# A gated MLP and a Mamba-2 mixer on one core: the skip weights' load, the order of the last stage, and four small moves

## The chip, the cores and the metric

The kernel runs on one core of one Trainium2 chip. The metric is the device time of one execution in microseconds (us). A core has five engines, each with its own queue of instructions that it works off in order: TensorE (PE; its weight loads are PEld), VectorE (DVE), ScalarE (ACT), GpSimd (POOL) and SyncE (SP). They wait for each other through semaphores. SP, ACT and POOL also issue DMA transfers.

## What is computed

Two layers over h of 1024 tokens by 1024 channels, then a last RMS norm. All is float32. The matmuls are split: each operand is written as a high and a low part, and three products (high times high, high times low, low times high) replace one.

```
h = x
# layer 0: chunked causal spatial gating
z, u, v = split(rmsnorm(h) @ a_w_in)            # 1024 -> 3 x 2048
mixed   = causal(w_s) applied per chunk of 128 to layernorm(v), + b_s
h       = h + (u * mixed * silu(z)) @ a_w_out
# layer 1: Mamba-2
z, xbc, dt = split(rmsnorm(h) @ b_w_in)         # 2048, 4096, 32 columns
x, B, C = split(silu(causal_conv(xbc)))         # 32 heads of 64, 8 groups of 128
dt      = softplus(dt + dt_bias);  dA = cumsum(dt * A) within each chunk
y       = diagonal part + part carried over chunks + x * d_skip   # d_skip: one number per head
h       = h + rmsnorm_per_group(y * silu(z)) @ b_w_out
out     = rmsnorm(h) * final_norm_w             # mean over 1024 channels, per token
```

## The kernel before

The kernel is one long program written out in order for all engines. In each stretch under `manual_schedule` every engine gets its instructions in the order of the code; where one stretch meets the next, instructions of both interleave. TensorE does nearly everything as blocks of 128x512 products.

**Seven products in place of eight.** Every large product is cut in four quarters and done with Strassen's form in Winograd's variant: seven products, numbered 1 to 7, of sums of the quarters. `Block` does this for columns of the two input projections, `Wide` for the columns of v, `Out` for the two output projections. The sums of weight quarters are `t1` and `t2` in `Block`; they are built by DMA transfers that add to their destination (`accum_op`), which POOL issues (`add`). `sums_a` starts `t2`, and `sums_b` goes on with `t1` and `t2`. Product 4 and 6 use `t2`, product 5 uses `t1`. `prep` casts an operand to its high part on ScalarE (`wh`, `xh`, `yh`) and subtracts on VectorE to get the low part (`wl`, `xl`, `yl`); `mm` multiplies; `post` takes the accumulators out of PSUM.

**First layer's start.** `head` normalizes x and does the first half of v's columns, `rest` the second. Between them some small parameters are loaded by SP: `hv` (decay bias and rate) and `dsk`, the skip weights of the 32 heads spread so that partition p holds head 2c + p//64 at column c. In `rest`, `mix_a` loads the mixing weights `ws`; `mix_b` transposes them on TensorE into `wc` (tag k2, four buffers, which the `vt` rows of v use too, until their stores to `v_d` have landed); `mix_c` multiplies ones by `wc` (L877). `mix_b` runs within the sixth product and `mix_c` ahead of the seventh.

**Decays.** `decays` is a generator. `blocks` calls it once in each unit of the second layer's projection, a unit being one of two halves of a product, until it ends. It holds VectorE's steps for softplus and the cumulative sums, ScalarE's exponentials, eight small stores by POOL, and four transposes on TensorE, among them those of `last`. Other work in a unit comes before its step.

**Output projections.** `Out.product` runs one of the products 1, 2, 7, 6, 4, 5 in four steps c of 24 matmuls; a hook adds the loads and sums of each step. `plus` sums on VectorE, `add` by a DMA. Rows are kept in halves of 512 channels, in `u`. `square` lets ScalarE sum the squares of a half row into `stats`. For the left half (nb 0), VectorE then scales that sum and adds the norm's small constant, one 128x1 step per row block (L1253). `rstd_half` and `rstd_a` add the right half's share, and POOL raises to the power -1/2; `rstd_b` refines it on VectorE. `ao` is the first layer's output, `bo` the second's.

**The end.** After product 5, `into_end` does product 3 of `bo` in four blocks of 24 matmuls, `last_mm(0)` to `last_mm(3)`, over operands that `prep_unit` splits. `post(3, tt)` adds the block to the rows (0, tt) and squares them. `finish_b(th, tt, rs)` scales the left half on ScalarE (already weighted, `weigh_left`), the right half on VectorE (with weights in the same step), and SP stores both. Rows (1, tt) were summed in product 5 and need only finishing, with `r1`.

Of the kernel before, what the change touches and what calls it, by code (L numbers as in the profile page):

```python
# [8 lines left out]
F32 = mybir.dt.float32  # L9
# [20 lines left out]
def kernel(  # L30
# [152 lines left out]
    class Block:  # L183
# [33 lines left out]
        def sums_b(self):  # L217
            nc.scalar.mul(self.t1, self.b[0, 0], -1.0)
            self.add(self.t1, 0, 1)
            self.add(self.t2, 1, 1)  # L220

# [606 lines left out]
    with tc.manual_schedule():  # L828
        second = head()
        hv = cst.tile([P, 4], F32, name="hv")  # L830
        nc.sync.dma_start(out=hv[0:32, 0:1], in_=b_dt_bias[0].rearrange("(h o) -> h o", o=1))
        for q in range(4):
            nc.sync.dma_start(out=hv[q * 32:(q + 1) * 32, 1:2], in_=b_a_log[0].rearrange("(h o) -> h o", o=1))
        dsk = cst.tile([P, 16], F32, name="dsk")
        dskv = b_d_skip[0].rearrange("(c f) -> f c", f=2)
        for f in range(2):
            nc.sync.dma_start(out=dsk[f * 64:(f + 1) * 64, :], in_=dskv[f].partition_broadcast(64))
        nA = hv[:, 2:3]
        nc.scalar.activation(nA, hv[:, 1:2], AF.Exp)
        nc.vector.tensor_scalar(nA, nA, -1.0, None, ALU.mult)  # L840
# [148 lines left out]
    class Out:  # L989
# [256 lines left out]
        def square(self, th, tt, nb):  # L1246
# [4 lines left out]
            nc.scalar.activation(junk, self.row(th, tt, nb), AF.Square, accum_out=ss[:, nb:nb + 1])  # L1251
            if nb == 0:
                nc.vector.tensor_scalar(ss[:, 0:1], ss[:, 0:1], 1.0 / D, NORM_EPS, ALU.mult, ALU.add)  # L1253

# [31 lines left out]
    def hook_a(n, c):  # L1286
# [11 lines left out]
        else:  # L1298
            ao.prep_last(c)
            store_h1(1, c, 0)  # L1300

# [280 lines left out]
    def decays():  # L1582
# [5 lines left out]
        yield  # L1588
        yield
        nc.scalar.activation(e_, e_, AF.Exp)  # L1590
        yield
# [31 lines left out]
        for q in range(4):  # L1623
# [4 lines left out]
            if q % 2:  # L1628
                yield
        tk = s8([P, 2048], "tk")  # L1630
        tok = tk[:, 0:768].rearrange("p (v c r) -> p v c r", v=3, c=2)
        decb = tk[:, 768:1024]
        last = k1([P, 256], "last")
        for j in range(2):
            nc.scalar.copy(out=last[:, j * P:(j + 1) * P],
                           in_=ecs[:, j * P + P - 1:j * P + P].broadcast_to([P, P]))
        tps = []
        for two in ((dt, dte), (cs, last)):
# [490 lines left out]
    def hook_b(n, c):  # L2129
# [18 lines left out]
        elif n == 2:  # L2148
# [12 lines left out]
            if c:  # L2161
                (bo.plus if c < 3 else bo.add)(bo.a(0, 0, c - 1), bo.a(1, 0, c - 1))
        elif n == 7:
# [28 lines left out]
        elif n == 5:  # L2192
            bo.prep_last(c)
            if c:
                weigh_left((c - 1) // 2, 2 * ((c - 1) % 2))
            if c == 3:
                bo.prep_unit(0)

    def finish_b(th, tt, rs):
        l, r = bo.row(th, tt, 0), bo.row(th, tt, 1)  # L2200
        nc.scalar.activation(l, l, AF.Identity, scale=rs)
        (nc.scalar if (th, tt) == (0, 3) else nc.sync).dma_start(out=outr[th * 4 + tt][:, 0:512], in_=l)
        nc.vector.scalar_tensor_tensor(r, r, rs, end["fnwb"][:, 512:], ALU.mult, ALU.mult)
        nc.sync.dma_start(out=outr[th * 4 + tt][:, 512:], in_=r)
# [226 lines left out]
    def into_end():  # L2431
# [5 lines left out]
        r1 = bo.rstd_half(1)  # L2437
        for tt in range(4):
            bo.last_mm(tt)
            if 0 < tt < 3:  # L2440
                bo.prep_unit(tt + 1)
            if tt:
                bo.post(3, tt - 1)
                bo.rstd_a(0, tt - 1)
            finish_b(1, tt, r1[:, tt:tt + 1])
            if tt:
                finish_b(0, tt - 1, bo.rstd_b(0, tt - 1))
        bo.post(3, 3)
        bo.rstd_a(0, 3)
        finish_b(0, 3, bo.rstd_b(0, 3))  # L2450

# [31 lines left out]
```

## Time and profile before

| what | value |
|---|---|
| runs | 1481.75, 1481.93, 1485.11 us (median 1481.93) |
| profiled execution | 1481.93 us, span from first to last instruction 1480.2 us |
| TensorE busy | 1452.0 us, 98% of the span, 7202 matmuls |
| VectorE, ScalarE, GpSimd busy | 1041.8 us (70%), 784.1 us (53%), 404.5 us (27%) |
| mean granted TensorE clock | 0.996 of full speed |
| DMA | 257.52 MB, mean 174 GB/s |

The profile is of one execution. Its page gives busy times, the chain of work that ended last, and the costliest groups of instructions. Further views answer questions: waits (who stood idle until whom), a timeline of one engine, windows (busy times in stretches of time), and the DMA issues with their times to landing. In a row, "[6.84 <-ACT wc L871]" means that the engine stood 6.84 us before this instruction and that the last thing it waited for was ScalarE's write of `wc` on line 871. Matmuls are pipelined, so their shown durations (0.39 us) overlap; the next starts after about 0.23 us.

### The profile page before, as it was taken

The page shows a single profiled execution, that of the slowest core. Times are in us where ns is not written, and L with a number is a line of the kernel's source. Part 1 is how long each engine was busy: PE and PEld are TensorE (multiplying, and loading weights), DVE is VectorE, ACT ScalarE, POOL GpSimd, SP SyncE. Part 2 cuts the span into 40 slices and gives each one's busy share as a digit, 9 for nine tenths or more (in the row PEclk, how much of TensorE's full clock was granted, in tenths as well). Part 3 has the DMA queues.
Part 4 walks back from the last instruction along what each step waited for, and adds up shares of the span by engine and source line. Part 5 has one row for each costly group of instructions (what it writes and reads, how often), then busy time and mean ns, then how long its engine had stood idle before and what let it go on. Part 6 is the DMA issues. An engine that isn't in the chain of part 4 may idle for free. (4 is left out here: it accounts for less than half of the span.)

```text
span 1480.2 us, 20005 instructions
## 1 busy us (share of the span) xinstructions
PE 1452.0 (98%) x7202; PEld 1196.5 (81%) x7202; DVE 1041.8 (70%) x1713; ACT 784.1 (53%) x1261; POOL 404.5 (27%) x451
## 2 busy tenths in 40 slices
PE   9998999999999999999999999999999999999997
PEld 7786888888888888887788888888888888787875
DVE  7864666776666655678665558767787777788976
ACT  7632333222323445565665646657677766866463
POOL 2101110000000023202122323205676767742221
PEclk9999999999999999999999999999999999999999
DMA  8653423332322999957467988786777566699963
GB/s 287 128 171 91 165 91 120 105 120 94 116 85 78 341 265 252 258 132 175 120 159 169 197 163 162 156 248 158 203 185 201 176 190 141 192 282 282 271 115 114
DMA packets 174549, 257.52 MB, mean 174 GB/s; under 512 B 16513, under 2 KB 98673, under 8 KB 171250
## 3 DMA queue, kind: packets, MB, share of 16 engines
q1 hardware_dynamic: 124128, 171.55, 37.7%
q0 software_dynamic: 42688, 70.79, 24.2%
q10 hardware_dynamic: 7634, 13.90, 2.6%
q8 instruction: 57, 0.93, 0.3%
q14 instruction: 42, 0.34, 0.1%
HBM read 187.19 MB, written 51.18 MB: 161 GB/s over the span
## 5 line engine op out<-in xcount | busy, mean ns | idle before, releaser
L134 PE MATMUL acc<-hh,wh 128*128 128x512 f32 x868 | 339.7, 391 | 0.7 <-ACT u L297 0.7
L136 PE MATMUL acc<-hh,wl 128*128 128x512 f32 x868 | 338.3, 390 | 0.4 <-DVE wl L112 0.3
L135 PE MATMUL acc<-hl,wh 128*128 128x512 f32 x868 | 337.8, 389 | 0.0
L136 PEld LDWEIGHTS acc<-hh,wl 128*128 128x128 f32 x868 | 162.9, 188 | 35.7 <-DVE wl L112 1.6
L134 PEld LDWEIGHTS acc<-hh,wh 128*128 128x128 f32 x868 | 163.1, 188 | 34.3 <-ACT u L297 1.1
L135 PEld LDWEIGHTS acc<-hl,wh 128*128 128x128 f32 x868 | 163.0, 188 | 33.0
L112 DVE TENSOR_TENSOR wl<-wr,wh 128x1024 fp32r<-128x1024 f32 (+1 forms) x81 | 96.2, 1188 | 105.8 <-ACT wh L111 105.6
L111 ACT CAST wh<-wr 128x1024 fp32r<-128x1024 f32 (+1 forms) x97 | 99.3, 1025 | 78.7 <-PE acc L135 58.7
L297 ACT COPY u<-acc 128x512 f32<-128x512 f32 x93 | 53.9, 582 | 148.0 <-PE acc L136 147.9
L134 PE MATMUL ab<-hh,wh 128*128 128x512 f32 x288 | 122.2, 424 | 0.0
L136 PE MATMUL ab<-hh,wl 128*128 128x512 f32 x288 | 113.2, 393 | 0.0
L135 PE MATMUL ab<-hl,wh 128*128 128x512 f32 x288 | 112.5, 391 | 0.6 <-DVE hl L112 0.6
L134 PE MATMUL acc<-wh,hh 128*128 128x512 f32 x216 | 85.6, 396 | 0.3 <-DVE vt L396 0.3
L135 PE MATMUL acc<-wl,hh 128*128 128x512 f32 x216 | 84.3, 390 | 1.0 <-DVE wl L364 1.0
L136 PE MATMUL acc<-wh,hl 128*128 128x512 f32 x216 | 84.1, 389 | 0.0
L976 POOL DMA_DIRECT2D y_d<-y x8 | 4.4, 550 | 287.2 <-DVE y L973 287.2
L1949 ACT ACTIVATE wl<-wl,tk 128x128 f32<-128x128 f32 x256 | 81.6, 392 | 0.3 <-DMA wl<-cs_d 0.2
L1967 DVE TENSOR_TENSOR wl<-wl,cw 128x512 f32<-128x512 f32 x64 | 61.0, 965 | 16.2 <-ACT wl L1951 15.1
L112 DVE TENSOR_TENSOR xl<-ya,xh 128x1024 fp32r<-128x1024 f32 x36 | 44.8, 1243 | 37.6 <-ACT xh L111 32.4
L1162 PE MATMUL bo<-wl,xh 128*128 128x512 f32 x192 | 64.2, 392 | 1.3 <-DVE stats L1253 0.7
L134 PEld LDWEIGHTS ab<-hh,wh 128*128 128x128 f32 x288 | 54.4, 189 | 13.3 <-issue 5.7
L111 ACT CAST xh<-ya 128x1024 fp32r<-128x1024 f32 x36 | 37.7, 1048 | 49.8 <-PE ao L1162 35.0
(331 smaller groups left out, 3236.4 us busy)
## 6 DMA issues: line engine op xcount, KB each, us to landing
wr<-in_a_w_in_dram SPq DMA_DIRECT2D x32, 512.0 KB, 3.6
wl<-cs_d SPq DMA_DIRECT2D x64, 256.0 KB, 5.4
wr<-in_b_w_in_dram SPq DMA_DIRECT2D x30, 512.0 KB, 4.3
wb<-in_a_w_out_dram SPq DMA_DIRECT2D x10, 1024.0 KB
wb<-in_b_w_out_dram SPq DMA_DIRECT2D x10, 1024.0 KB, 9.4
wr<-in_b_w_in_dram SPq DMA_DIRECT2D x36, 256.0 KB, 5.3
wide<-in_a_w_in_dram SPq DMA_DIRECT2D x16, 512.0 KB, 7.3
v<-v_d SPq DMA_DIRECT2D x8, 1024.0 KB
```

The costliest lines, as they stand in the source:

```text
L111: nc.scalar.copy(out=hi, in_=src)
L112: return (eng or nc.vector).tensor_tensor(out=lo, in0=src, in1=hi.bitcast(F32), op=ALU.subtract)
L134: nc.tensor.matmul(out=o, lhsT=l[0], rhs=r[0], start=start, stop=False, **kw)
L135: nc.tensor.matmul(out=o, lhsT=l[0], rhs=r[1], start=False, stop=False, **kw)
L136: nc.tensor.matmul(out=o, lhsT=l[1], rhs=r[0], start=False, stop=stop, **kw)
L297: nc.scalar.copy(out=self.u[n][:, i], in_=a)
L976: store = lambda: nc.gpsimd.dma_start(out=y_d[-1], in_=y)
L1162: nc.tensor.matmul(out=o[i], lhsT=X[x_][:, k, i * P:(i + 1) * P], rhs=Y[y_][:, k, :], start=not more and c == 0 and k == 0 and x_ == y_, s ...
L1949: nc.scalar.activation(wl[:, j, :], wl[:, j, :], AF.Relu, scale=-1.0, bias=tokc(2, c, self.g)[:, j:j + 1])
L1967: V.tensor_tensor(out=wl, in0=wl, in1=self.cw[c][:, 640:768].unsqueeze(1).broadcast_to([P, 4, P]), op=ALU.mult)
```

## The change

Six places change.

1. `sums_b` issues the second sum into `t2` before the sum into `t1`.
2. The skip weights come as one row of 32 numbers, broadcast to all partitions (`skip`), and two VectorE copies take every second one into `dsk`, instead of two DMA loads.
3. In `Out`, the scaling of the left half's mean is one step for four row blocks (`mean`), called in the second and third step of product 5, instead of one step per row block.
4. `decays` waits one unit more before its first exponential, and copies `last` one unit before the transposes; its two temporary tiles are allocated a unit later.
5. In the second product of `bo`, the sum of the third step goes by DMA (`add`) instead of on VectorE (`plus`), as that of the fourth does.
6. `into_end` is written out without its loop, with another order of the finishing, squaring and splitting, and the last right half is multiplied by the norm's weights before its root is known.

```diff
         def sums_b(self):
             nc.scalar.mul(self.t1, self.b[0, 0], -1.0)
+            self.add(self.t2, 1, 1)
             self.add(self.t1, 0, 1)
-            self.add(self.t2, 1, 1)
...
+        skip = cst.tile([P, 16, 2], F32, name="skip")
+        nc.sync.dma_start(out=skip.rearrange("p c f -> p (c f)"), in_=b_d_skip[0].partition_broadcast(P))
         dsk = cst.tile([P, 16], F32, name="dsk")
-        dskv = b_d_skip[0].rearrange("(c f) -> f c", f=2)
         for f in range(2):
-            nc.sync.dma_start(out=dsk[f * 64:(f + 1) * 64, :], in_=dskv[f].partition_broadcast(64))
+            nc.vector.tensor_copy(out=dsk[f * 64:(f + 1) * 64, :], in_=skip[f * 64:(f + 1) * 64, :, f])
...
             nc.scalar.activation(junk, self.row(th, tt, nb), AF.Square, accum_out=ss[:, nb:nb + 1])
-            if nb == 0:
-                nc.vector.tensor_scalar(ss[:, 0:1], ss[:, 0:1], 1.0 / D, NORM_EPS, ALU.mult, ALU.add)
+
+        def mean(self, th):
+            v = stats[:, th * 4:th * 4 + 4, int(self.keep), 0]
+            nc.vector.tensor_scalar(v, v, 1.0 / D, NORM_EPS, ALU.mult, ALU.add)
...
             ao.prep_last(c)
+            if c in (1, 2):
+                ao.mean(c - 1)
...
         yield
         yield
+        yield
         nc.scalar.activation(e_, e_, AF.Exp)
...
-        tk = s8([P, 2048], "tk")
-        tok = tk[:, 0:768].rearrange("p (v c r) -> p v c r", v=3, c=2)
-        decb = tk[:, 768:1024]
         last = k1([P, 256], "last")
...
+        yield
+        tk = s8([P, 2048], "tk")
+        tok = tk[:, 0:768].rearrange("p (v c r) -> p v c r", v=3, c=2)
+        decb = tk[:, 768:1024]
         tps = []
...
-                (bo.plus if c < 3 else bo.add)(bo.a(0, 0, c - 1), bo.a(1, 0, c - 1))
+                (bo.plus if c < 2 else bo.add)(bo.a(0, 0, c - 1), bo.a(1, 0, c - 1))
...
             bo.prep_last(c)
+            if c in (1, 2):
+                bo.mean(c - 1)
...
-        nc.vector.scalar_tensor_tensor(r, r, rs, end["fnwb"][:, 512:], ALU.mult, ALU.mult)
+        if weighed is None:
+            nc.vector.scalar_tensor_tensor(r, r, rs, end["fnwb"][:, 512:], ALU.mult, ALU.mult)
+        else:
+            nc.vector.tensor_scalar(r, weighed, rs, None, ALU.mult)
...
-        for tt in range(4):
-            bo.last_mm(tt)
-            if 0 < tt < 3:
-                bo.prep_unit(tt + 1)
-            if tt:
-                bo.post(3, tt - 1)
-                bo.rstd_a(0, tt - 1)
-            finish_b(1, tt, r1[:, tt:tt + 1])
-            if tt:
-                finish_b(0, tt - 1, bo.rstd_b(0, tt - 1))
+        bo.last_mm(0)
+        bo.prep_unit(2)
+        bo.last_mm(1)
+        bo.post(3, 0)
+        bo.rstd_a(0, 0)
+        finish_b(1, 0, r1[:, 0:1])
+        bo.prep_unit(3)
+        finish_b(0, 0, bo.rstd_b(0, 0))
+        bo.last_mm(2)
+        bo.post(3, 1)
+        finish_b(1, 1, r1[:, 1:2])
+        bo.rstd_a(0, 1)
+        finish_b(1, 2, r1[:, 2:3])
+        finish_b(0, 1, bo.rstd_b(0, 1))
+        bo.last_mm(3)
+        bo.post(3, 2)
+        bo.rstd_a(0, 2)
+        finish_b(1, 3, r1[:, 3:4])
+        finish_b(0, 2, bo.rstd_b(0, 2))
         bo.post(3, 3)
+        left = k2([P, 512], "left")
+        nc.vector.tensor_tensor(out=left, in0=bo.row(0, 3, 1), in1=end["fnwb"][:, 512:], op=ALU.mult)
         bo.rstd_a(0, 3)
-        finish_b(0, 3, bo.rstd_b(0, 3))
+        finish_b(0, 3, bo.rstd_b(0, 3), left)
```

More of the change, by code (lines that the diff above doesn't have):

```diff
@@ L2197, in hook_b, with finish_b @@
                 bo.prep_unit(0)
-    def finish_b(th, tt, rs):
+    def finish_b(th, tt, rs, weighed=None):
         l, r = bo.row(th, tt, 0), bo.row(th, tt, 1)
```

## The prediction, made before the change was run

> **What bounds the kernel now.** I read the page's busy shares, then the stages, then TensorE's waits, then the queues around the longest of them.
>
> ```profile
> PE 1452.0 (98%) x7202; PEld 1196.5 (81%) x7202; DVE 1041.8 (70%) x1713; ACT 784.1 (53%) x1261; POOL 404.5 (27%) x451
> ```
> ```profile
> 100.00:200.00 100.00, 93.16 (x405) 75.38 (x405) 65.82 (x122) 29.77 (x42) 16.95 (x22) 0.97 0.38 126
> ```
> ```profile
> PE tp L877 <- ACT wc L871: 6.8, 1, 6.8
> ...
> PE bo L1162 <- DVE stats L1253: 0.7, 1, 0.7
> ...
> PE acc L134 <- ACT u L297: 0.7, 1, 0.7
> ...
> PE bo L1162 <- DVE wl L1069: 0.4, 1, 0.4
> PE tp L1643 <- ACT last L1635: 0.4, 1, 0.4
> ...
> PE acc L136 <- DVE wl L112: 0.3, 1, 0.3
> ```
>
> TensorE is busy for 1452.0 of 1480.2 us, so only what it stands idle, what it runs at a lower clock, and what follows its last matmul can be won; an instruction saved elsewhere counts only where TensorE waits for it. One stretch stands out, 100 to 200 us, with 6.84 us idle and a mean clock of 0.97. The waits name 6.8 us at once at the matmuls of `mix_c` (L877); each other wait that the change touches is under 1 us. What follows the last matmul is read below, at the part on the end.
>
> Around L877, in the order of the queues (SP, POOL, ACT, DVE, PE), and the DMA beside it:
>
> ```profile
> 117.40 1.40 SPq L837 DMA_DIRECT2D dsk<-in_b_d_skip_dram  x2
> ```
> ```profile
> 123.78 0.69 POOL L397 DMA_DIRECT2D v_d<-vt  x1 [0.69 <-DVE vt L396]
> ```
> ```profile
> 139.75 1.23 ACT L871 COPY wc<-tp 128x512 f32<-128x512 f32 x2 [20.62 <-DMA v_d<-vt]
> ```
> ```profile
> 141.97 1.22 DVE L364 TENSOR_TENSOR wl<-wide,wh 128x1024 fp32r<-128x1024 f32 x1 [15.43 <-ACT wh L360]
> ```
> ```profile
> 127.06 1.03 PE L869 MATMUL tp<-ident,ws 128*128 128x128 f32 x8
> ...
> 132.94 0.39 PE L135 MATMUL acc<-wl,hh 128*128 128x512 f32 x1
> 133.16 0.39 PE L136 MATMUL acc<-wh,hl 128*128 128x512 f32 x1
> 140.39 3.73 PE L877 MATMUL tp<-wc,ones 128*128 128x512 f32 x4 [6.84 <-ACT wc L871]
> ...
> 144.19 0.40 PE L135 MATMUL acc<-wl,hh 128*128 128x512 f32 x1
> ```
> ```profile
> 137.00:139.00 2.00, 0.00 (x0) 0.00 (x0) 0.00 (x0) 0.00 (x0) 0.00 (x0) 0.53 0.79 301
> ```
> ```profile
> 118.80:137.00 18.20, 14.75 (x70) 11.96 (x68) 7.60 (x15) 0.20 (x1) 2.82 (x4) 1.00 0.05 0
> ```
> ```profile
> v_d<-vt POOLq DMA_DIRECT2D x4, 256.0 KB, 19.1
> ...
> hv<-in_b_a_log_dram SPq DMA_DIRECT2D x4, 0.1 KB, 2.1
> ```
> ```profile
> v_d<-vt POOLq DMA_DIRECT2D x16, 256.0 KB, 3.2
> ```
>
> The windows give the share of the DMA engines and GB/s last, the clock ahead of them. SP issues the skip weights' two loads at 117.4 to 118.8: 4 KB each, but source elements that do not lie side by side, so 2 x 64 x 16 = 2048 pieces of 4 bytes. From 118.8 to 137 the DMA engines are busy for a share of 0.05 and move 0 GB/s to the digit. The four 256 KB stores of `vt` that POOL issues by 124.5 take 19.1 us to land; over the whole run such a store takes 3.2. `wc` is written over the buffers of these `vt` (tag k2), so ScalarE stands 20.62 us, copies at 139.75, and TensorE, out of work at about 133.4, starts L877 at 140.39, at a clock of 0.50 from about 137.
>
> **The change, part by part.**
>
> *The skip row.* Two loads of 4-byte pieces go; one load of 128 rows of 128 bytes (32 heads, side by side) and two VectorE copies of 64x16 come. The nearest row for such pieces is the load of the 32 decay columns at L1365, 1024 pieces of 128 bytes:
>
> ```profile
> DMA packets 1073, 0.16 MB, mean 127 GB/s; under 512 B 1040, under 2 KB 1073, under 8 KB 1073
> ```
>
> 1040 packets under 512 B, those 1024 among them, pass in a window of 1.3 us; a short load lands 2.1 us after its issue (`hv` above). So the row, issued near 118, lands by 118 + 2.1 + 1.3 = 121.4. The stores then land at 124.5 + 3.2 = 127.7, the transposes before `wc` end at 128.1, and both copies (1.23) are done by 129.4, 4 us before TensorE comes to L877. Its next matmul is due at 133.16 + 0.23 (the pitch of the two rows at 132.94 and 133.16) = 133.39; from L877 to the second matmul of the product takes 144.19 - 140.39 = 3.80 at clock 0.50, so 1.9 at 1.00; 144.19 - (133.39 + 1.9) = **8.9 us**. What could be late next is the seventh product's weights, which VectorE had to delay for the same wait; ScalarE and VectorE are free for it from 129.4 on, instead of 141, with L877 and the product's first half (24 matmuls, 5.4 us) ahead of its use. The two copies cost nothing, since VectorE has nothing to do from 126.5 on (it stood 15.43 us until 141.97); if the row is late they hold back the sums queued behind them, of which some 3 us of lateness are covered by that idle time, and beyond it TensorE's transposes at 127.06 wait. Bounds: 0 (the loads are not the cause) to 8.9.
>
> A rule bears on this. The Trainium skill, "DMA: Bandwidth & Descriptors", section "Queues, rings and completion order", says that each DMA engine takes turns between its queues packet by packet. By that rule POOL's stores would slip between the 4-byte pieces, the 19.1 us would have another cause, and this part would bring 0; the trace does not agree, since 0 GB/s moved while four stores stood issued.
>
> *Order of the sums (`sums_b`).* POOL now adds the second half into `t2` before `t1`. `t2` feeds the sixth product, `t1` the fifth, a product or more later. The price is the wait of 0.3 at L136, where ScalarE's cast of `t` had waited for its DMA: gain **0.3**, bounds -0.5 to 0.7; if `t1` were late, ScalarE's copy for the fifth product would stand, with at least one whole product in front of it. On POOL the sum into `t1` now stands behind the wait for the first half of `t2` to land, as that of `t2` stood behind ScalarE's copy before.
>
> *The decays' steps.* One step later, Exp no longer precedes the copy that frees the accumulator:
>
> ```profile
> 746.64 1.28 ACT L1590 ACT_TABLE_LOAD   x1
> 747.93 0.42 ACT L1590 ACTIVATE dtw<-dtw 128x256 f32<-128x256 f32 x1
> ...
> 749.19 1.06 ACT L297 COPY u<-acc 128x512 f32<-128x512 f32 x2
> ```
>
> The copy at 749.19 stands behind a table load and Exp (1.28 + 0.42), and L134 waits 0.7 for it; a unit later, it goes ahead of them. `last` is copied one unit ahead of its transposes, which waited 0.4. With them POOL's eight stores of the sums move by one unit; only the scans read them, much later. Sum 1.1; since every later step moves by a unit, and Exp of the sums brings a second table load before another copy, I take **0.8**, bounds -1.5 to 1.3.
>
> *Means of the half rows.* Sixteen 128x1 steps of VectorE go, four of 128x4 come, of about the same 0.15 us (first row below). In the second output each old step also makes VectorE wait for ScalarE's square:
>
> ```profile
> 1424.50 0.15 DVE L1253 TENSOR_SCALAR stats<-stats 128x1 f32<-128x1 f32 x1 [0.79 <-ACT junk L1251]
> ...
> 1427.72 0.15 DVE L1253 TENSOR_SCALAR stats<-stats 128x1 f32<-128x1 f32 x1 [0.85 <-ACT junk L1251]
> ...
> 1429.81 1.22 DVE L112 TENSOR_TENSOR wl<-wb,wh 128x1024 fp32r<-128x1024 f32 x1
> ```
>
> Three of them (first and last shown) stand 0.79 to 0.85 each ahead of the `wl` at 1429.81, for which TensorE waits (0.7, put down to `stats`). Without them VectorE's sums close up and ScalarE's squares follow one another: about 1.1 us earlier, so the 0.7 goes, and part of two shorter gaps after it. **1.1**, bounds 0 to 1.6. In the first output TensorE does not wait there: 0.
>
> *One more sum by DMA.* `plus` (1.14 us of VectorE) at the third step of the second product becomes an added transfer of 512 KB. It frees the `wl` at L1069 for which TensorE waits 0.4. But that stretch is full:
>
> ```profile
> 1359.00:1362.00 3.00, 3.00 (x15) 2.49 (x14) 2.90 (x8) 1.91 (x2) 0.16 (x1) 1.00 1.09 218
> ```
> ```profile
> 1364.40 1.06 ACT L111 CAST xh<-ya 128x1024 fp32r<-128x1024 f32 x1 [3.49 <-DMA ya<-ya]
> ```
> ```profile
> 1354.39 0.90 POOL L1086 DMA_DIRECT2D wb<-wb  x1
> ```
> ```profile
> 1364.60 1.98 PE L1162 MATMUL bo<-wh,xh 128*128 128x512 f32 x8
> ```
> ```profile
> DMA to landing us min/median/max: 5.4/8.7/10.7
> ```
>
> The share is 1.09, and the next such sum already lets ScalarE stand 3.49. POOL can issue the new one at about 1354.4, where the next sum of weights goes now; landing takes 5.4 to 10.7 us. Its operand is wanted by TensorE's block of 1364.60, less the 0.4, and two casts of 1.06 by ScalarE come first, so it must land by 1362.1: at 7.7 us it is just in time, at 10.7 TensorE waits 3.0. Behind it on POOL stand the sums for later products, each later by up to 2.4 us (512 KB at the row's 218 GB/s). The middle landing, 8.7, would cost 1.0 and give 0.4 back; but VectorE, freed of 1.14, makes the sum's other operand earlier, so **0**, bounds -2.6 to +0.4.
>
> *The end.* VectorE's and ScalarE's queues are reordered; the rows before:
>
> ```profile
> 1455.65 0.16 DVE L153 TENSOR_TENSOR rh<-rr,ru 128x4 f32<-128x4 f32 x1
> ...
> 1464.24 0.68 DVE L1232 TENSOR_TENSOR u<-bo,u 128x512 f32<-128x512 f32 x1
> ...
> 1472.45 0.68 DVE L1232 TENSOR_TENSOR u<-bo,u 128x512 f32<-128x512 f32 x1
> 1473.98 0.16 DVE L1265 SCALAR_TENSOR_TENSOR stats<-stats 128x1 f32<-128x1 f32 x1 [0.85 <-ACT junk L1251]
> ```
> ```profile
> 1475.49 0.72 ACT L2201 ACTIVATE u<-u,stats 128x512 f32<-128x512 f32 x1 [1.55 <-DVE stats L153]
> ```
> ```profile
> 1469.86 0.39 PE L136 MATMUL bo<-yh,wl 128*128 128x512 f32 x1
> ```
>
> TensorE's four last blocks (24 matmuls, 5.45 us each at the 0.227 us of the eight in 1.98 above, the last of these 0.39 long) follow without a gap and end at 1470.25, so the second was done at 1459.4; yet its sum runs at 1464.24, since the third and fourth blocks' splits and two roots stand ahead of it, and the two sums behind it come 4.1 us apart, to 1472.45: a chain of sum, square, POOL's power, root and scaled halves. In the new order block three's splits follow `r1` (1455.65 + 0.16), two operations of a sum's size (0.68): the sum of block 0 starts at 1457.2. One chain of 4.1 later comes that of block 1, plus block four's two splits where POOL's power does not cover them: 1461.3 to 1462.7, then two chains: 1469.5 to 1470.9. TensorE allows 1470.25. Between these I take 1470.45, as the splits are mostly covered: 1472.45 - 1470.45 = **2.0**, bounds 0 and 2.2. If the casts of block four came late, TensorE would stand: they start when the square of block 0 is done, near 1459, and are wanted at 1464.8. The right half's weights, now multiplied ahead (0.68), fill VectorE's 0.85 wait before 1473.98; the right half's last step becomes cheaper, but ScalarE's left half still ends at 1475.49 + 0.72 in the old count, and its store after it, so 0, at best 0.3.
>
> **Sum.** 8.9 + 0.3 + 0.8 + 1.1 + 0 + 2.0 = 13.1. The profiled execution took 1481.93 us, 1.73 more than its span, and is the median of the three runs itself: 1481.93 - 13.1 = **1468.8**.
>
> **The rivals.**
> *The added sum is late.* Worked out above, -2.6; for it speak the share of 1.09 and the 3.49, against it that two of the three marks of its landing are below 9. Then 1481.93 - 10.5 = 1471.4.
> *The small parts bring nothing.* The end stays tied by its chain, and the decays meet another copy: only 8.9, 0.3 and 1.1 remain: 1471.6.
> *The long wait has another cause,* as by the rule above: 13.1 - 8.9 = 4.2, so 1477.7. Against it: 301 GB/s move from 137 on, when the pieces end.
> *Slower.* The row comes through as slowly as the old pieces and lands at 138, as those do. VectorE stands from about 121 (an estimate of the copies' place, from the issue and the landing); the sums behind that free the accumulators need some 2.5 us (two sums of 0.68, two statistics of about that size) and end at 140.5; the transposes of 127.06 wait for them; the 5.4 us of matmuls between them and L877 take 3.0 more at half clock (a mean of 0.97 over 100 us is some 6 us at 0.50), L877 1.9: the matmul of 144.19 comes at 150.8, 6.6 later. With the other 4.2 that is 1481.93 + 2.4 = 1484.3. It decides from a landing at about 135.6 on, where 6.6 falls to 4.2; the 1.3 us for 1024 pieces speaks against it.
>
> **How the numbers follow.** Forecast 0.72 (own range 1466 to 1471); late sum 0.09; small parts nothing 0.09; other cause 0.05; slow row 0.03; something not foreseen, above 1486.4, 0.02. A change under 0.3% (4.4 us) cannot be told from none. Faster: 0.90 and 0.02 of "other cause", whose 1477.7 lies at that border, so 0.92; same: 0.03 and 0.02 of the slow row, whose +2.4 is inside, so 0.05; slower: 0.02 and 0.01, so 0.03. The range: at the low end all upper bounds (8.9 + 0.7 + 1.3 + 1.6 + 0.4 + 2.2 + 0.3 = 15.4, 1466.5) and 1.2 us for gaps that I did not follow, 1465.3; at the high end the first two rivals with 0.9 to spare, 1472.5.
>
> **What would show it.** The skip row: no 0.05 stretch after 118 us, `wc` copied near 128, L877 at 133.4 at clock 1.00. The decays: no wait of L1643 for `last`, none of L134 for `u` near 749. Means: L1253 gone, no wait at 1431 less the shift. The added sum: a wait of ScalarE for `ya` ahead of the second step of the seventh product, followed by one of TensorE or not. The end: the last sum within 0.3 us of TensorE's end. The prediction is wrong if L877 still waits, or if new waits of TensorE after 700 us exceed 3 us.

## Result and the profile after

The changed kernel takes **1465.99 us** (median of four runs, 1464.51 to 1467.45), the kernel before on the same chips 1481.84 (1481.41 to 1485.11). The ratio is 0.9888, with a 95% interval from 0.9871 to 0.9904: about 15.9 us less, where 13.1 were forecast. The profiled execution took 1464.71 us, with a span of 1463.0.

The page's busy shares, the window of the stage, and the longest waits of TensorE between its start-up and the end:

```profile
PE 1446.2 (99%) x7202; PEld 1195.3 (82%) x7202; DVE 1040.4 (71%) x1703; ACT 783.6 (54%) x1261; POOL 405.0 (28%) x452
```
```profile
100.00:200.00 100.00, 100.00 (x444) 82.17 (x443) 70.61 (x131) 34.52 (x48) 16.93 (x22) 1.00 0.40 132
```
```profile
PE ab L135 <- DVE hl L112: 1.6, 1, 1.6
...
PE bo L1163 <- ACT wh L1069: 0.8, 2, 0.5
```

TensorE does the same 7202 matmuls in 5.8 us less busy time (1446.2 against 1452.0); between 100 and 200 us it stands for nothing (100.00 busy, clock 1.00, before 93.16 and 0.97). The wait of 6.8 for `wc` is gone, and no wait of its size has come. The longest one now, 1.6 for `hl` between 963 and 1005 us, was 0.6 before; it is 1.5 in experiment 1 and absent in experiments 2 and 7, so it goes with no edit.

The queues around `mix_c` (now L878), in the order SP, DVE, POOL, ACT, PE, and the issues from 115 to 128 us:

```profile
115.62 0.42 SPq L835 DMA_DIRECT2D skip<-in_b_d_skip_dram  x1
```
```profile
119.54 0.49 DVE L838 COPY dsk<-skip 64x16 f32<-64x16 f32 x2
```
```profile
122.48 0.69 POOL L397 DMA_DIRECT2D v_d<-vt  x1 [0.69 <-DVE vt L396]
```
```profile
125.87 1.07 ACT L872 COPY wc<-tp 128x512 f32<-128x512 f32 x2 [8.49 <-PE tp L870]
```
```profile
131.58 1.88 PE L878 MATMUL tp<-wc,ones 128*128 128x512 f32 x4
...
133.53 0.40 PE L135 MATMUL acc<-wl,hh 128*128 128x512 f32 x1
```
```profile
v_d<-vt POOLq DMA_DIRECT2D x4, 256.0 KB, 2.6
...
skip<-in_b_d_skip_dram SPq DMA_DIRECT2D x1, 16.0 KB, 3.0
```

One load of 16 KB (128 rows of 128 bytes) lands 3.0 us after its issue, the two VectorE copies take 0.49 together, the four stores of `vt` land after 2.6 instead of 19.1, ScalarE copies `wc` 14 us earlier, after a wait for TensorE's own transposes instead of a DMA, and TensorE comes from the product into L878 without a pause, at full clock.

The places of the other parts (DVE at the second output's product 5; then the end on DVE, ACT and PE; then ScalarE where the decays' Exp had stood ahead of a copy):

```profile
1415.25 1.22 DVE L112 TENSOR_TENSOR wl<-wb,wh 128x1024 fp32r<-128x1024 f32 x1
...
1423.40 0.17 DVE L1256 TENSOR_SCALAR stats<-stats 128x4 f32<-128x4 f32 x1
```
```profile
1442.46 0.68 DVE L1233 TENSOR_TENSOR u<-bo,u 128x512 f32<-128x512 f32 x1
...
1455.84 0.69 DVE L1233 TENSOR_TENSOR u<-bo,u 128x512 f32<-128x512 f32 x1
1456.56 0.69 DVE L2471 TENSOR_TENSOR left<-u,fnwb 128x512 f32<-128x512 f32 x1
```
```profile
1458.89 0.72 ACT L2210 ACTIVATE u<-u,stats 128x512 f32<-128x512 f32 x1 [1.55 <-DVE stats L153]
```
```profile
1455.39 0.39 PE L136 MATMUL bo<-yh,wl 128*128 128x512 f32 x1
```
```profile
736.94 0.57 ACT L297 COPY u<-acc 128x512 f32<-128x512 f32 x1
737.53 1.28 ACT L1596 ACT_TABLE_LOAD   x1
```

Four means are one step of 0.17 us. The first block's sum comes at 1442.46 (the forecast's 1457.2, less the 14.5 by which this kernel is ahead there, would be 1442.7); the last sum (L1233) starts at 1455.84, with TensorE's last matmul ending at 1455.39 + 0.39 = 1455.78; the right half is weighted at 1456.56, while ScalarE squares. `u` is copied at 736.94, ahead of the table load.

**Where the 17.2 us of span went.** Both kernels run the same matmuls, so the n-th of one can be set beside the n-th of the other. Below, each stretch runs from one matmul to another of the same number (times of the changed kernel), and the figure is what it takes longer than in the changed kernel, worked out from the starts of the matmuls in the traces; the last column is from the last matmul's start to the end of the span, itself.

| kernel | start, to 15 us | 131 to 143, `mix_c` | 725 to 790, decays | 790 to 861, sums order | 963 to 1005 | 1318 to 1371, added sum | 1371 to 1453, means | tail |
|---|---|---|---|---|---|---|---|---|
| before | 1.66 | 8.82 | 1.10 | 0.56 | -1.02 | 0.92 | 1.86 | 10.35 |
| after | 0 | 0 | 0 | 0 | 0 | 0 | 0 | 7.61 |
| before, skip row only | 0.01 | 0.00 | 2.83 | 0.93 | -0.02 | 0.09 | 1.89 | 10.13 |
| before, pieces behind | 1.89 | 0.01 | 1.29 | 0.79 | -1.73 | 0.89 | 1.87 | 10.36 |
| before, 1536 pieces | 0.01 | 5.01 | 1.43 | 0.70 | -1.67 | 0.56 | 1.89 | 10.50 |
| after, skip undone | 2.57 | 9.37 | -0.29 | 0.00 | -1.73 | 1.31 | 0.01 | 8.03 |
| after, end undone | 2.71 | 0.00 | 0.83 | 0.00 | -1.48 | 0.76 | -0.02 | 10.15 |
| after, means undone | 1.81 | 0.00 | -0.37 | 0.00 | -0.65 | 1.07 | 1.87 | 7.64 |
| after, sum undone | 2.57 | 0.00 | -0.24 | 0.00 | -2.44 | 0.79 | -0.02 | 7.63 |
| after, decays undone | 2.38 | 0.00 | 2.36 | 0.00 | -0.58 | 0.95 | -0.02 | 7.63 |
| after, `left` undone | 2.72 | 0.00 | 0.64 | 0.00 | -1.16 | 1.08 | -0.01 | 8.05 |
| after, one sum more | 2.11 | 0.00 | -0.52 | 0.00 | -1.18 | 2.91 | -0.05 | 7.65 |
| after, order undone | 2.75 | 0.00 | 0.41 | 0.79 | -0.84 | 0.78 | 0.01 | 7.63 |
| after, Exp's unit undone | 0.00 | 0.00 | 1.79 | 0.00 | -1.10 | 0.77 | -0.02 | 7.65 |

The columns in which the values fall into two groups by one edit are what that edit is worth. Three columns do not: the start, where the time until TensorE's matmuls follow at full pace varies by 0 to 2.75 with no edit that goes with it; 963 to 1005; and that of the added sum (0.09 to 0.92 without it, 0 to 1.31 with it). Stretches that are not listed (among them 15 to 131, 861 to 963 and 1005 to 1318) hold a few tenths in most rows, 1.2 to 1.4 in two places each of "pieces behind" and "1536 pieces", and once 3.5 (the last row, from 45 to 55 us; the last section says why). Experiments 3 and 4 are not in the table.

### The profile page after: what moved, and what is told of

Read it like the earlier page. It is cut to its first block, busy times and chain, and to the rows that moved or that the text cites. A ratio compares the mean times of both kernels' runs of the same rounds, so it can differ in the third digit from the quotient of the medians.

```text
span 1463.0 us, 19994 instructions
## 1 busy us (share of the span) xinstructions
PE 1446.2 (99%) x7202; PEld 1195.3 (82%) x7202; DVE 1040.4 (71%) x1703; ACT 783.6 (54%) x1261; POOL 405.0 (28%) x452
## 5 line engine op out<-in xcount | busy, mean ns | idle before, releaser
L1974 DVE TENSOR_TENSOR wl<-wl,cw 128x512 f32<-128x512 f32 x64 | 61.0, 965 | 15.9 <-ACT wl L1958 14.8
L1163 PE MATMUL bo<-wh,xh 128*128 128x512 f32 x192 | 63.3, 393 | 0.8 <-ACT wh L1069 0.8
```

The lines of the kernel that those rows point to most:

```text
L1163: nc.tensor.matmul(out=o[i], lhsT=X[x_][:, k, i * P:(i + 1) * P], rhs=Y[y_][:, k, :], start=not more and c == 0 and k == 0 and x_ == y_, s ...
L1974: V.tensor_tensor(out=wl, in0=wl, in1=self.cw[c][:, 640:768].unsqueeze(1).broadcast_to([P, 4, P]), op=ALU.mult)
```

## The experiments

The first four ask what held the stores; the next four each undo one small part; then four that separate what these left open, and two on the last terms. Times of kernels without an interval are of one run.

**1. The row alone.**

```diff
 # kernel before
-        for f in range(2):
-            nc.sync.dma_start(out=dsk[f * 64:(f + 1) * 64, :], in_=dskv[f].partition_broadcast(64))
+        nc.sync.dma_start(out=skip.rearrange("p c f -> p (c f)"), in_=b_d_skip[0].partition_broadcast(P))
+        for f in range(2):
+            nc.vector.tensor_copy(out=dsk[f * 64:(f + 1) * 64, :], in_=skip[f * 64:(f + 1) * 64, :, f])
```

> Only the skip row of the change; everything else as before. Theory (2048 pieces of 4 bytes pass one after another and nothing else passes beside them, so the stores that wc waits for are late): 8.9 us less than before, about 1473, the stores of vt land in some 3 us, L877 starts within 0.5 us of the end of the sixth product, at full clock. Rival (the stores are late for another cause, since the DMA engines take turns between queues): within 1 us of before, L877 still about 7 us late.

1474.43 us (1473.07 to 1474.61), ratio 0.9936 (0.9919 to 0.9953): 9.3 less than the kernel before in the runs beside it (1483.7), and 8.8 less in the stretch of `mix_c`. In the decays' stretch the old waits were longer in this profile (2.83 against 1.10).

**2. The row taken out of the changed kernel** (the same lines the other way).

> The change with the two old loads of the skip weights back. Theory: 8.9 us more than the change, about 1475, and the wait of L877 is back at 6 to 7.5 us. Rival (the stores are late for another cause): as the change, about 1466. If the skip row's worth depends on the other parts, the step at L877 differs from that of the kernel with the skip row alone.

1476.94 us (1476.46 to 1478.36), ratio to the kernel before 0.9954 (0.9939 to 0.9969). The wait is back whole, and the stretch is 9.37 longer. TensorE's waits:

```profile
PE tp L877 <- ACT wc L871: 6.8, 1, 6.8
```

**3. Twice the pieces.** Two more loads of the same form into a tile that nothing reads.

```diff
 # kernel before, behind the loads of dsk
+        more = cst.tile([P, 16], F32, name="more")
+        for f in range(2):
+            nc.sync.dma_start(out=more[f * 64:(f + 1) * 64, :], in_=dskv[f].partition_broadcast(64))
```

> The kernel before with both loads of the skip weights issued twice, the second time into a tile that nothing reads: 4096 pieces of 4 bytes in place of 2048. Theory: the stretch without traffic doubles, from some 19 to some 39 us, ending near 157; L877 starts near 160 and the time rises by 19 to 21 us, to about 1502. Rival (the length of the stretch has nothing to do with the pieces): within 2 us of before.

1488.3 us, 4.6 more than the kernel before in the runs beside it, where 19 to 21 were expected. Set against the profile of the kernel before, the span is 6.4 longer, of which 4.5 had gone by 55 us, where nothing is changed, and only 1.0 at `mix_c`. TensorE's wait there, then SP's issues, and two windows that follow each other (share of the DMA engines and GB/s last):

```profile
PE tp L880 <- ACT wc L874: 7.6, 1, 7.6
```
```profile
121.89 1.40 SPq L837 DMA_DIRECT2D dsk<-in_b_d_skip_dram  x2
123.33 11.29 SPq L840 DMA_DIRECT2D more<-in_b_d_skip_dram  x2
```
```profile
122.00:141.00 19.00, 16.04 (x75) 13.03 (x73) 8.87 (x16) 0.20 (x1) 2.81 (x4) 1.00 0.05 0
141.00:161.00 20.00, 15.40 (x55) 11.27 (x56) 10.08 (x21) 8.08 (x13) 2.17 (x4) 0.83 0.19 57
```

Doubling the pieces did not double the hold; that expectation failed. SP needed 11.29 us to issue the second pair, where the first took 1.40. In the trace the second pair passes from about 141 on, at the same 106 pieces per us, and now the stores, which POOL had issued at 124.1 to 128.9, pass beside it. So what seems to count is how many pieces were handed over ahead of the stores, and not how many there are in all; experiments 9 and 10 test this.

**4. The pieces on another queue.** The same two loads, issued by ScalarE.

```diff
 # kernel before
-            nc.sync.dma_start(out=dsk[f * 64:(f + 1) * 64, :], in_=dskv[f].partition_broadcast(64))
+            nc.scalar.dma_start(out=dsk[f * 64:(f + 1) * 64, :], in_=dskv[f].partition_broadcast(64))
```

> The kernel before with the two old loads issued by ScalarE's queue in place of SP's. Theory (the DMA engines themselves are held by the pieces, whichever queue they come from): as before, about 1482, stretch of 0.05 share and some 19 us for the stores of vt. Rival (only what shares SP's queue or its making of descriptors is held): the stores land in some 3 us and the time falls by about 9, to 1473.

1490.06 us, where 1482 was expected: worse, and at another place. ScalarE issues them earlier, at 111.95, and now SP's own small loads of `hv` land 18.2 us after their issue (2.1 before), and SP needs 7.97 us to issue the four of them (2.12 before); VectorE stands 16.44 for `hv`, and TensorE 11.6 for the `vt` behind it. The issues, VectorE's timeline, and TensorE's waits:

```profile
hv<-in_b_a_log_dram SPq DMA_DIRECT2D x4, 0.1 KB, 18.2
```
```profile
137.50 0.15 DVE L840 TENSOR_SCALAR hv<-hv 128x1 f32<-128x1 f32 x1 [16.44 <-ACT hv L839]
```
```profile
PE tp L869 <- DVE vt L396: 11.8, 2, 11.6
```

The hold therefore reaches over queues: pieces on ScalarE's hold loads on SP's, as those on SP's held stores on POOL's.

**5. The end undone** (the loop of the kernel before in `into_end`, and `finish_b` without `left`).

> The change with the old end: the loop, and the last right half weighted in its last step. Theory: from TensorE's last matmul to the last instruction 2 to 3 us more than in the change (7.6 there), so 1468 to 1469; the last sum into the rows comes 2 us after TensorE's end, behind VectorE's queue. Rival (the end was shortened by the means' earlier work on VectorE, not by the order): within 0.5 us of the change.

1469.72 us (1468.32 to 1470.73), ratio 0.9907 (0.9893 to 0.9922). The tail is 10.15 instead of 7.61, so 2.5. The means are in place here, so it is not they that shortened the end.

**6. The means undone** (one step per row block in `square` again, without `mean`).

> The change with a mean's step per row block again, in both outputs. Theory: VectorE stands for ScalarE's squares again, TensorE loses 1.5 to 2.1 us in three gaps at the start, in the middle and at the end of the fifth product of the second output, and nothing in the first output: about 1468. Rival (the order at the end or the added sum made these gaps go): the gaps stay away, time as the change.

1468.58 us (1467.0 to 1469.29), ratio 0.9897 (0.988 to 0.9914). The stretch is 1.87 longer. That of the first output, within 143 to 725 us, took the same within 0.01: all of it is the second's.

**7. The added sum undone.**

```diff
 # changed kernel
-                (bo.plus if c < 2 else bo.add)(bo.a(0, 0, c - 1), bo.a(1, 0, c - 1))
+                (bo.plus if c < 3 else bo.add)(bo.a(0, 0, c - 1), bo.a(1, 0, c - 1))
```

> The change with the third step's sum on VectorE again. Theory: the gap of 0.6 us in the last step of the second product comes back, with some 0.3 beside it: 0.9 us more than the change, 1467. Rival (the added transfer costs time later in the seventh product, which now goes): 0.5 to 1 us less than the change.

1465.7 us (1465.64 to 1466.84), ratio 0.9883 (0.9868 to 0.9897), against 0.9888 (0.9871 to 0.9904) of the changed kernel: no difference that could be seen, where 0.9 more was expected. The waits tell why. First this kernel, then the kernel of experiment 5, which has the added sum, both from 1330 to 1375 us:

```profile
PE bo L1163 <- DVE wl L1070: 0.4, 1, 0.4
```
```profile
PE bo L1163 <- DVE wl L112: 0.4, 1, 0.4
```

On VectorE the sum makes TensorE wait 0.4 in the second product in three of the five kernels of the table that have it there (not in experiments 1 and 10); by DMA that wait is gone, and in seven of the eight profiles with one such sum a wait of 0.3 to 0.6 comes in the seventh product instead, behind ScalarE's wait for `ya`. The changed kernel's own profile is the one without it.

**8. The decays undone** (Exp a unit earlier, `last` copied with its transposes).

> The change with the decays' steps as before. Theory: the waits near 738 us (for the copy of u, 0.7) and near 767 (for last, 0.4) come back, 1.1 us more than the change up to 800 us, and the waits between 970 and 1000 us, longer in the change than before, stay as they are in the change, since they hang on transfers. Rival (those later waits, 1.0 and 0.8 us longer, are the price of the later steps): they fall back to their length before, and the time is the change's within 0.5 us.

1467.75 us (1466.78 to 1470.07), ratio 0.9897 (0.9882 to 0.9912). The stretch is 2.36 longer than in the changed kernel, more than the 1.1 expected. Between 963 and 1005 its value (-0.58) lies among those of the kernels with the new steps (-2.44 to 0), so no price of the later steps is seen there. The waits for `u` and `last` are back, and one of 0.5 for `wl` with them.

**9. The pieces behind the stores.** All 2048 stay, but ScalarE issues them after its copies of `wc`.

```diff
 # kernel before
-        for f in range(2):
-            nc.sync.dma_start(out=dsk[f * 64:(f + 1) * 64, :], in_=dskv[f].partition_broadcast(64))
...
     def mix_b():
         for h in range(2):
...
+        for f in range(2):
+            nc.scalar.dma_start(out=dsk[f * 64:(f + 1) * 64, :], in_=dskv[f].partition_broadcast(64))
```

> The kernel before with its two loads of 4-byte pieces kept, but issued by ScalarE's queue behind its copies of wc (so behind POOL's four stores of vt). Theory: the pieces (2048 at 9.4 ns, about 20 us) hold only what is issued after them. Then the stores land in about 3 us, wc is copied near 126, the matmuls of mix_c stand for nothing and the offset against the kernel before is -8 to -9 there: 1474 to 1477 us, as the load of v and the first loads of wr, issued behind the pieces, start up to 3 us late and may cost that. In the trace: 4-byte pieces at about 106 per us from about 127 to 147, and no other large transfer until they are through. Rival A: the pieces slow whatever is under way, whenever issued; the stores still take over 10 us and the time stays at 1480 to 1484. Rival B: the twenty us of hold only move to the next transfers and come back in full there (v, wr): again 1480 to 1484, with the wait of TensorE after 140 in place of that at 133.

1473.63 us (1472.92 to 1475.14), ratio 0.9939 (0.9922 to 0.9955): as much as the row alone (0.9936). The windows behind the issue at 128.44, and the issues from 117 to 160 us:

```profile
124.00:128.00 4.00, 4.00 (x22) 3.36 (x21) 2.84 (x4) 0.00 (x0) 0.69 (x1) 1.00 0.36 124
129.00:136.00 7.00, 7.00 (x29) 5.12 (x28) 1.76 (x2) 4.22 (x7) 0.98 (x2) 1.00 0.04 0
136.00:142.00 6.00, 6.00 (x28) 4.96 (x27) 6.00 (x19) 0.00 (x0) 1.08 (x2) 1.00 0.28 91
142.00:148.00 6.00, 6.00 (x28) 4.95 (x28) 2.32 (x2) 4.16 (x7) 0.00 (x0) 1.00 0.04 0
```
```profile
addb_d<-ab POOLq DMA_DIRECT2D x2, 512.0 KB, 16.9
wcT_d<-wc POOLq DMA_DIRECT2D x2, 256.0 KB, 11.4
```

The `vt` stores are through by 128; then the pieces take the next twenty us, and the stores behind them take 11.4 and 16.9 us to land, but nobody waits for those. Rival B falls as well: the hold is a delay of transfers, and costs only where someone waits for them. Nor is the hold complete: from 136 to 142 some 90 GB/s of stores pass among the pieces.

**10. Three quarters of the pieces.** 12 columns in pieces, four from a row.

```diff
 # kernel before
+        skip = cst.tile([P, 16, 2], F32, name="skip")
+        nc.sync.dma_start(out=skip.rearrange("p c f -> p (c f)"), in_=b_d_skip[0].partition_broadcast(P))
...
+        dsk2 = cst.tile([P, 4], F32, name="dsk2")
-            nc.sync.dma_start(out=dsk[f * 64:(f + 1) * 64, :], in_=dskv[f].partition_broadcast(64))
+            nc.sync.dma_start(out=dsk[f * 64:(f + 1) * 64, :], in_=dskv[f, 0:12].partition_broadcast(64))
+            nc.vector.tensor_copy(out=dsk2[f * 64:(f + 1) * 64, :], in_=skip[f * 64:(f + 1) * 64, 12:16, f])
```

> The kernel before with 12 of the 16 columns loaded in 4-byte pieces (1536 instead of 2048) and the last four taken from a row load, as in the changed kernel. Theory: the hold is the number of pieces at 9.4 ns, so it ends 4.8 us earlier: wc is copied near 135 instead of 139.75 (less the start's luck of up to 2.5), TensorE waits about 2.2 instead of 6.8 at mix_c, and since the clock fell only after about 3.6 us of standing, mix_c and the product's first matmuls run at full clock: 6.5 to 7 us gained there of the 9, a time of 1475.5 to 1478. Rival A: the hold belongs to the form of the load, not to the number of its pieces: nothing gained, 1481 to 1484. Rival B: gain in proportion to the pieces alone, with the clock still low: 4.8, 1477 to 1479, and matmuls of mix_c 0.9 us apart instead of 0.43.

1478.6 us (1476.43 to 1479.84), ratio 0.9974 (0.9964 to 0.9983): 4 us, as Rival B has it. The timeline of ScalarE, TensorE's wait, and two windows (clock third from the end):

```profile
135.48 0.59 ACT L875 COPY wc<-tp 128x512 f32<-128x512 f32 x1 [16.99 <-DMA v_d<-vt]
```
```profile
PE tp L881 <- ACT wc L875: 3.1, 1, 3.1
```
```profile
135.00:136.00 1.00, 0.00 (x0) 0.00 (x0) 0.00 (x0) 0.52 (x1) 0.00 (x0) 1.00 0.99 279
137.00:138.00 1.00, 1.00 (x2) 0.62 (x2) 0.06 (x1) 1.00 (x2) 0.54 (x1) 0.50 0.56 209
```

`wc` is copied at 135.48 instead of 139.75: 4.3 earlier, where 512 pieces at 9.4 ns are 4.8; the pieces are issued at 117.40 in both kernels, and the other 0.5 is not accounted for. So the number of pieces sets the hold, and the form of the load alone does not. The clock fell all the same, to 0.50 by 137, after a stand of only 3.1 us; my guess that this would spare it was wrong.

**11. `left` undone** (the last right half weighted and scaled in one step).

> The changed kernel without the multiplication ahead: the last right half is scaled and weighted in one step, as before. Read only from the last matmul's start to the span's end: 7.61 in the changed kernel, 10.35 in the kernel before. Theory: the right half's store is issued 0.27 us earlier with it, and the last store's landing counts, so the tail is 7.9 to 8.2 without it. Rival: the left half on ScalarE ends last in both, so the tail stays at 7.6.

1469.01 us; the tail is 8.05, 0.44 longer, as expected. In the kernel before and here, both stores of the last rows are issued within 0.03 us of each other; in the changed kernel the right half's is issued 0.24 ahead of the left half's and 0.29 earlier than here, and the last packet passes 0.29 earlier, counted from TensorE's last matmul. The other 0.15 lies behind the packets and is not explained.

**12. One more sum by DMA.**

```diff
 # changed kernel
-                (bo.plus if c < 2 else bo.add)(bo.a(0, 0, c - 1), bo.a(1, 0, c - 1))
+                (bo.plus if c < 1 else bo.add)(bo.a(0, 0, c - 1), bo.a(1, 0, c - 1))
```

> The changed kernel with one more sum of the second product (its second step) by a transfer that adds, none left on VectorE. Theory: the landing of these sums is already just in time (ScalarE's cast of xh stands 3.0 to 4.5 us for ya in every run, and TensorE 0.5 to 0.7 behind it in most), so 512 KB more ahead of them at about 218 GB/s make TensorE wait 1 to 2.5 us more at the seventh product: 1467 to 1468.5, tail and start unchanged. Rival: VectorE's 1.14 us set the pace there and come free: 0 to 0.6 us gained, 1465.4 to 1466.

1469.47 us (1468.48 to 1471.06), ratio 0.9913 (0.9898 to 0.9928): 3.5 slower than the changed kernel. The stretch is 2.9 longer than in the changed kernel's own profile and 2.1 longer than the mean of the kernels with one such sum, where 1 to 2.5 were expected. TensorE now waits for casts of `wh` too; they stand on ScalarE behind casts of `xh` that wait for `ya`, one of them shown last:

```profile
PE bo L1163 <- ACT wh L111: 1.1, 2, 0.7
...
PE bo L1163 <- DVE wl L112: 0.6, 1, 0.6
```
```profile
1357.72 1.05 ACT L111 CAST xh<-ya 128x1024 fp32r<-128x1024 f32 x1 [4.43 <-DMA ya<-ya]
```

**13. The order of the sums undone** (the sum into `t1` first in `sums_b`).

> The changed kernel with the sum into t1 ahead of the second sum into t2 again. Read from the stretch between the 3640th and the 3950th matmul (790 to 860 us), which took the same within 0.04 in every kernel with the new order. Theory: the order alone brings back TensorE's wait for wl, and each matmul that waits loses 0.1 to 0.2 more than the wait shown: 0.5 to 0.95 us longer there. Rival: part of it belongs to the decays, which end shortly before: 0.1 to 0.4.

1469.38 us; the stretch is 0.79 longer, as the four other kernels of the table with the old order had it (0.56 to 0.93), and 0.00 in all with the new one. It is the order alone.

**14. Exp's unit undone** (one `yield` less; `last` still copied a unit ahead).

> The changed kernel with the unit before the first exponential taken out again, while last is still copied a unit ahead of its transposes. Read from the waits and the stretch between the 3350th and the 3640th matmul (725 to 790 us). Theory: the two halves are separate waits: TensorE waits for the copy of u again (0.7 to 0.9 shown, 0.86 to 1.05 lost), and not for last; the stretch is 0.7 to 1.3 longer than the mean of the kernels with the new steps. Rival: the unit by itself does it, as it moves all later steps too: the wait for last (0.4 to 0.5) and that for wl (0.5) come back with it, 1.8 longer.

1469.93 us. The waits, and the two matmuls around the first of them:

```profile
PE acc L134 <- ACT u L297: 0.9, 1, 0.9
PE acc L136 <- DVE wl L112: 0.5, 1, 0.5
```
```profile
741.86 0.39 PE L136 MATMUL acc<-hh,wl 128*128 128x512 f32 x1
743.11 0.50 PE L134 MATMUL acc<-hh,wh 128*128 128x512 f32 x1 [0.87 <-ACT u L297]
```

The wait for `u` is back, that for `last` is not: they are separate. The stretch is 1.7 longer than the mean of the kernels with the new steps, more than the 0.7 to 1.3 expected, as a wait for `wl` came too; that one comes in about half the profiles with the new steps, so this run cannot give it to either.

## Where the prediction held, and the step of it that failed

The direction, the cause of the long wait and the rank of the parts held; the sum was 13.1 and the median moved 15.9 (14.2 to 19.1 by the interval of the ratio). What failed is the sizing of the sum's small terms. With the edits' own runs, the order of the sums is worth 0.8 (forecast 0.3, upper bound 0.7), the decays 1.7 (0.8, 1.3), the means 1.9 (1.1, 1.6) and the end 2.5 (2.0, and 2.2 + 0.3): 6.9 in place of 4.2, each at its upper bound or above it. The step behind the first three is that a wait of TensorE was entered at about the size that the list of waits shows, or below it; the spacing of the matmuls shows more, as worked out below. The range was too narrow at that end: 1465.99 lies just below the forecast's own range (1466 to 1471) and below the sum of all upper bounds (1466.5), and the profiled execution, 1464.71, lies below 1465.3 too. Only the 1.2 us that the prediction set aside for gaps it did not follow keeps the median inside.

The four runs of the changed kernel lie in two pairs, 1464.5 to 1464.7 and 1467.3 to 1467.5, with the median between them. Their distance is like the spread of the start's column, for which the last section gives the clock as the reason. That it is the reason here too is likely but not shown, since one of the four runs was profiled.

The steps, by stretches:

| step | forecast | before to after | with the edit's own runs |
|---|---|---|---|
| skip row | 8.9 | 8.8 | 8.8 (1), 9.4 (2) |
| order of the sums | 0.3 | 0.6 | 0.8 (13) |
| decays | 0.8 | 1.1 | 1.7 (mean of the table's five with the old steps less mean of eight with the new, experiment 14 in neither) |
| means | 1.1 | 1.9 | 1.9 (6) |
| added sum | 0 | 0.9 | 0 (7); means of the profiles 0.65 without, 0.84 with |
| end | 2.0 | 2.7 | 2.5 (5) |
| sum | 13.1 | 16.0 | 15.7 to 16.3 |

The pair of profiles adds 1.7 at the start, takes back 1.0 between 963 and 1005, and some 0.6 lies in stretches not listed: 17.2 of span. These are not the change's: other kernels show them in both directions without it.

*The skip row* was right in its mechanism and its size (8.9 against 8.8). What the prediction read from one stretch (nothing passes beside the pieces) is shown by experiments 1, 2, 9 and 10 to be the cause, and by 3 and 9 to be not quite so: transfers issued behind the pieces wait, those issued ahead do not, and some pass later on.

The rule weighed there, from the Trainium skill, "DMA: Bandwidth & Descriptors", section "Queues, rings and completion order", is that each DMA engine takes turns between its queues, packet by packet. By that rule alone experiment 4's `hv` should have landed near its 2.1 us; it took 18.2, so the rule alone does not describe these pieces. The 90 GB/s among the pieces from 136 to 142 in experiment 9 are the part of it that was seen. The long issues on SP (11.29 us in experiment 3, 7.97 in experiment 4) show that handing transfers over was held up too. What holds them inside the DMA system the traces do not show, and it stays open.

*The means* are the small term whose error is measured best: 1.9 in the pair of profiles, in experiment 6 and in three others. The reading that failed is "the 0.7 goes, and part of two shorter gaps after it". All three gaps of TensorE went. In the kernel before they stood at 1431.08, 1437.02 and 1448.21, and the matmuls' starts there lie 0.87, 0.38 and 0.40 us further apart than the usual 0.23: 1.65, and 0.2 in matmuls around them. VectorE's work on product 5 was one chain through ScalarE's squares. In the kernel before, the `wl` of 1429.81 ends at 1431.03, just ahead of the matmul at 1431.08 that waits for it; in the changed kernel that `wl` ends at 1415.25 + 1.22 = 1416.47, and the matmul of the same number starts at 1417.63. VectorE is 1.2 ahead there, and the two operands that were late after it no longer are.

*The waits were taken at their shown size,* and that was too little at each of them. Experiment 14 shows it in two rows: a wait shown as 0.9, but 743.11 - 741.86 = 1.25 between the starts, 1.02 more than 0.23. A wait is counted from the end of the matmul before, 0.39 after its start, while the next could have started after 0.23: so 0.16 more is lost. The order's 0.3, the decays' 0.7 and 0.4 and the means' 0.7 all carry it, and below the list's size are gaps that are not listed.

*The decays:* 1.1 was read, 0.8 taken, for a second table load that might hold another copy. It held none: the sum of two gaps lost, 0.86 and 0.51 in the kernel before, is 1.37, and the profiles' means differ by 1.7. The single profiles scatter (1.10 to 2.83 with the old steps, -0.52 to 0.83 with the new), so the 1.7 is good to a few tenths only.

*The added sum* came out as worked: just in time, the gain of 0.4 and a new wait of about its size. The 0.9 of the pair is luck of that profile. Experiment 12 shows that the next one is too late, at 2.1 more than the mean with one, near the price of the first rival (2.6).

*The end:* the last sum starts 0.06 us after TensorE's end (forecast 0.2); the four sums lie 5.2, 4.1 and 4.1 us apart, as the prediction's chain had them (4.1 to 5.5, 4.1 and 4.1). "So 0, at best 0.3" for the multiplication ahead failed: experiment 11 gives 0.44, most of it through the two stores. I had looked at which engine ended last, not at what their stores do to each other.

## What to carry to other kernels

Count a load's pieces, not its bytes: 2048 pieces of 4 bytes, 8 KB in all, held the transfers that other engines issued behind them for some 18 us, in one run with a part of them let through, and either a row that is spread on chip or another place in the order of issues takes that away. The price of a wait is the distance between the starts of two matmuls less the usual one, not the wait that a list shows, and small waits in a chain go together when one link goes. A transfer that is just in time in one profile should be read in several: its wait comes and goes.

## What was not expected of the hardware

- Pieces of 4 bytes pass at 9.4 ns each (106 per us) with the DMA engines at a share of 0.05, whichever of two queues issued them; the 16 KB row of 128-byte pieces landed in 3.0 us.
- TensorE's clock came up at different times after the start. In the traces' records of the granted clock, full clock begins at 10.35 to 10.59 us in four of the table's 14 profiles and at 14.24 to 16.53 in the other ten, with no edit that goes with it; the transposes at L460 follow each other by 0.21 us before that moment and by 0.11 after it. Half of the delay against the changed kernel (10.51) is 1.9 to 3.0 us, and the start's column shows 1.66 to 2.75, always 0.2 to 0.3 less, so the clock accounts for that column. The Trainium skill, "TensorE: Matmul & The Clock Gate", Part 1 (the clock gate), describes a window of about 3.4 us that runs free of the program. The traces agree: where the clock fell in the course of a kernel, it stayed down for 3.41, 6.83 or, in experiment 4, 13.65 us. A shift by up to one such window at half pace would cost up to 1.7, an estimate from the page's figure; the shift seen is up to 6.2 us, nearly two of them.
- The clock fell after a stand of 3.1 us (experiment 10), about 0.7 us after TensorE had started again, and came back 3.4 us later. It fell after shorter stands too: in experiment 14 TensorE stood 0.7 us at 46 and 1.8 us until 50.19 (0.9 in the changed kernel), and the half clock is on record from 51.55 to 54.97. These waits and that clock make up the 3.5 of the table's last row.
